# Two-layer DiT block on one core: modulation steps redistributed, first FFN weights prepared during the output projection, two more buffers where the down projection leaves its accumulators

## The chip, the cores and the metric

One core of a Trainium2 chip runs the whole forward pass as one program. The metric is the device time of that program in microseconds (us), the median of the runs shown. Engines are named as in the profile: PE (TensorE, with its weight loads PEld), DVE (VectorE), ACT (ScalarE), POOL (GpSimd), SP (SyncE, here the queue that issues nearly all DMA transfers). L12 is line 12 of the kernel before.

## What is computed

The reference is two transformer layers on 1024 tokens of width 1024 plus, in layer 0, 256 context tokens. A conditioning vector gives six modulation vectors a layer (`mod = silu(c) @ w_mod + b_mod`): shift, scale and gate of the mixer, shift, scale and gate of the FFN.

```python
for li in range(2):
    sh1, sc1, ga1, sh2, sc2, ga2 = split(silu(c) @ w_mod[li] + b_mod[li], 6)
    u = rmsnorm(h, g_norm1[li]) * (1 + sc1) + sh1
    y = mixer(u)                              # layer 0: RG-LRU + MLA, layer 1: differential attention
    h = h + ga1 * y                           # y ends with the output projection
    u = rmsnorm(h, g_norm2[li]) * (1 + sc2) + sh2
    a, g = split(u @ w_up, 2)                 # 1024 -> 2 x 2816
    h = h + ga2 * ((gelu(dwconv(g)) * a) @ w_down)
# layer 0 does the same for the context tokens, with modulation from c_ctx
```

## The kernel before, in words

Every product is made in split precision: an operand is cut into a rounded high part (a CAST on ACT, L284) and the rest (a subtraction on DVE, L99), and `mm3` (L114) issues three matmuls for one (lines 117, 118, 119). So each new weight costs ACT about one us and DVE about 1.2 us before PE can use it.

**Output projection** (`out_proj`, L790). Ten token tiles of 128 rows in layer 0 (context first), eight in layer 1. Per tile: 48 matmuls (`ops`), times the gate vector `ga` on DVE (L825), plus the residual on POOL (L826), stored; then, some stages later (`norm`, L833), the RMS norm (`scaled`: square on ACT, power on POOL L127, scaling on POOL L261), eight transposes on PE (`turned`, L271) and the writing of the FFN's input columns. Both `ga` vectors are loaded at the start (L800). In layer 0 two modulation chunks (10 and 11 of layer 0, the FFN's gate) are computed here on DVE, 16 multiply-adds each (L195). At the last tile `fill` calls `begin`: in layer 0 `ctx_first` (L964) makes the context's products of FFN tiles 0 and 1, in layer 1 `first_products` (L973) one product each for tiles 0 and 1 from half weights.

**Up projection** (`ffn_up`/`up_sequence`, L999, L1009). 22 tiles f of 128 hidden columns. The 1024 input rows and 1024 tokens are cut 2 x 2, and seven products of 12 matmuls replace eight: p1, E with operand 22, p6 (operand t2), E with t1, B with t3, A with 21, B with t4. This stretch is in `manual_schedule`: every engine gets its instructions in the order in which the code emits them. Tile 0 stands ahead of the loop (L1068 to L1102): it fetches and splits its weights, makes the weight sums (`up_sums`, L985, four DVE additions), and splits the operands t2, t1, t3, 21, t4, 22 (L910), each two casts on ACT and two subtractions on DVE. The context's two products (24 matmuls each, `pC`) are made per tile in layer 0.

**Modulation steps.** `mod_chunk_dve` (L169) with `fine` is cut into six steps per chunk (`mod_steps`, L1153): clear the accumulator and issue the first load; four times multiply-add a loaded [128, 1024] piece of `w_mod` (L195: four instructions with both conditioning vectors, two with one) and issue the next load into the same single buffer `mr`; then the sum over partitions on PE (L205 or L212) and a copy. In layer 0's up projection nine chunks, that is 54 steps, hang in a list; `some_mods` takes one step at two places of each loop pass f = 1 to 21 (L1128 behind E with t1, L1138 behind B with t3), and `while mods` (L1150) takes the rest behind the loop. Three chunks more go into layer 0's down projection.

**Down projection** (`ffn_down`, L1158). Rounds of up to four token tiles; in a round PE accumulates 22 weights for each tile in PSUM (`acc`). At the end of a round DVE multiplies each accumulator with the gate into `dtmp` (L1232, two buffers), POOL adds the residual (L1233), and the result is stored. The next round needs the same accumulators and split weights.

**Layer 1's front** (`layer1_front`, L1241). Six weight blocks in turn, ten token tiles each (`project`, 24 matmuls). Tiles 0 to 6 were normed in the down projection; tiles 7 to 9 are loaded (`load`), scaled (`scale`) and transposed (`norm`) here, at lags 0, 1 and 3 of a staggered loop in which `project` has lag 4.

Outside `manual_schedule` the order within an engine is set by a planner at build time, by the order of emission and its own estimate of when operands are ready. The `p2` banks of PSUM are one pool of four for products, transposes and the context's products.

Of the kernel before, what the change touches and what calls it, by code (L numbers as in the profile page):

```python
# [34 lines left out]
OMODS = (0, 3, 4, 7)  # L35
# [25 lines left out]
class K:  # L61
# [107 lines left out]
    def mod_chunk_dve(self, pool, l, ch, nctx, fine=False):  # L169
# [31 lines left out]
        ps = [self.PS.tile([P, 512], F32, tag="mp", bufs=1, name="modps")] if self.single else self.two("modps")  # L201
# [588 lines left out]
    def out_proj(self, l, w_name, tiles, get_yT, begin, units=()):  # L790

        nc, io = self.nc, self.io
        with ExitStack() as st:
# [6 lines left out]
            gas = [self.ga(O, l, 0, c, f"ga{c}") for c in range(2 if l == 0 else 1)]  # L800
# [4 lines left out]

            mods = [self.mod_chunk_dve(O, 0, ch, 2) for ch in (10, 11)] if l == 0 else []

            def mod(t):
                if mods and t in OMODS:
                    next(mods[OMODS.index(t) // 2], None)  # L810

            def product(t):
# [12 lines left out]
                nc.vector.tensor_mul(h[t], ps.rearrange("p a b -> p (a b)"), gas[t >= NTX])  # L825
                nc.gpsimd.tensor_tensor(h[t], h[t], xt, op=ADD)  # L826
# [20 lines left out]
            self.staggered(tiles, (load, 0), (product, 1 + l), (fill, LAG_N + l), (norm, LAG_N + l), (mod, 1))  # L847
# [67 lines left out]
    def fetch_up(self, l, f):  # L915
        raws = []
        for i in (f, NF + f):
# [46 lines left out]
    def ctx_first(self, F, n):  # L964

        for f in range(n):
            a, g = (self.split_new(x) for x in self.fetch_up(0, f))
# [5 lines left out]
    def first_products(self, F, n):  # L973

        for f in range(n):
            raw = self.W.tile([P, 1024], F32, tag="wr", bufs=NWR, name="wr")[:, :512]
            self.nc.sync.dma_start(raw, self.io["ffn_up"][1, f, :, :512])
            w = self.split_new(raw, F, "pw", 1)
            ps = self.two("p1")[0]
            for k in range(4):  # L980
                self.mm3(ps, [y[:, k * P:(k + 1) * P] for y in w], [y[:, k] for y in self.right["11"]], k == 0, k == 3)
# [17 lines left out]
    def ffn_up(self, l, F0, nfirst, chunks):  # L999


        with ExitStack() as st:
            self.PS = self.ps(st, f"psU{l}")
            self.single = True
            with self.tc.manual_schedule():
                self.up_sequence(l, st, nfirst, chunks)
            self.single = False

    def up_sequence(self, l, st, nfirst, chunks):  # L1009
# [7 lines left out]
        step, mods = {}, []  # L1017
# [81 lines left out]
        N["raw"] = self.up_sums(B, raws)  # L1099
# [3 lines left out]
        mods += [x for ch in chunks for x in self.mod_steps(F, 1, ch, 2 if ch < 4 else 1)]  # L1103
        for f in range(1, NF + 1):
# [17 lines left out]
            here = l == 0 and f >= nfirst  # L1122
# [5 lines left out]
            some_mods()  # L1128
            if here:
                cgc = self.ctx_gate(F, f, X["c"][:, :CTX])  # L1130
            if f + 1 < NF:
                N = step[f + 1] = {"a": self.split_new(raws[0])}
                if l == 0 and f + 1 >= nfirst:
                    N["a21"] = self.split_new(raws[1][:, h], F, "a21", 1)
                N["raw"] = self.up_sums(B, raws)
# [579 lines left out]
```

## Time and profile before

| | |
|---|---|
| runs | 3 |
| median | 3470.52 us |
| lowest to highest | 3469.31 to 3471.54 us |
| the profiled execution | 3466.52 us |
| its span, first to last instruction | 3464.7 us |
| granted TensorE clock, mean | 0.968 |
| bytes moved | 435.64 MB, mean 126 GB/s |

The profiled execution's time is 1.8 us more than its span, and 4.0 us below the median. A row of a timeline has the start, the duration, the engine, line, operation and operands, how many were merged, and in brackets how long the engine had been idle and who released it. The stages on the timeline: attention of layer 0 to 731, output projection 740 to 889, up projection to 1466, a stretch behind its loop to 1523, down projection to 1860, layer 1's front to 2220, attention to 2640, output projection to 2764, up projection to 3212, down projection to the end.

### The profile page before, as it was taken

What the parts mean: (1) busy time and instruction counts of PE and PEld (TensorE: products, weight loads), DVE (VectorE), ACT (ScalarE), POOL (GpSimd) and SP (SyncE); (2) the same over time, 40 slices, a digit from 0 to 9 for tenths busy, and PEclk for the clock granted to TensorE, in tenths of its full rate; (3) what the DMA queues carried; (4) which work ended last, traced back from release to release, by engine and by line L of the source; (5) the groups of instructions that cost most, each with busy time, mean ns of one, the idle gap of its engine ahead of it and who ended that gap; (6) DMA issues with size and microseconds to landing.
All of it is one profiled execution on the core that took longest, in us unless ns stands there. A gap on an engine that the chain in (4) does not pass through costs nothing.

```text
span 3464.7 us, 43470 instructions
## 1 busy us (share of the span) xinstructions
PE 3173.4 (92%) x16262; PEld 2625.9 (76%) x16262; DVE 2365.8 (68%) x3380; ACT 1417.1 (41%) x2447; POOL 948.2 (27%) x658
## 2 busy tenths in 40 slices
PE   8998899989799999949997999888888889999998
PEld 4877788867588888738775887777777768888887
DVE  6468978876777766633666487499997676766443
ACT  3355766733333333212243122377764333333322
POOL 2233578864000000000022133177774300000010
PEclk9999999999899999969998999999999989999999
DMA  6224943354122222244754354644324222222553
GB/s 258 69 76 137 291 126 96 81 162 154 51 104 94 104 90 84 88 152 151 264 185 163 110 140 104 182 111 113 101 82 142 73 67 79 86 79 88 189 173 128
DMA packets 232874, 435.64 MB, mean 126 GB/s; under 512 B 21548, under 2 KB 147756, under 8 KB 230872
## 3 DMA queue, kind: packets, MB, share of 16 engines
q1 hardware_dynamic: 230792, 426.06, 38.8%
q10 hardware_dynamic: 1872, 6.82, 0.5%
q8 instruction: 128, 2.10, 0.2%
q14 instruction: 82, 0.67, 0.1%
HBM read 321.46 MB, written 111.34 MB: 125 GB/s over the span
## 4 chain that ended last, share of the span: by engine, by line
PE 54%; DVE 12%; issue 7%; DMA 3%; ACT 2%; POOL 1%; SPq 0%; DVEq 0%; ACTq 0%; POOLq 0%
PE pB L118 5%; PE pB L117 5%; PE pB L119 5%; PE acc L119 3%; PE pj L117 3%; PE pj L118 3%; PE pj L119 3%; PE acc L117 3%; PE acc L118 3%; DVE m L1453 2%; DVE p L1469 2%; PE pE L118 2%; PE pE L119 2%; PE pE L117 2%; PE ops L118 2%
## 5 line engine op out<-in xcount | busy, mean ns | idle before, releaser
L99 DVE TENSOR_TENSOR wl<-wr,wh 128x1024 fp32r<-128x1024 f32 (+2 forms) x288 | 351.2, 1229 | 95.5 <-ACT wh L284 70.6
L119 PE MATMUL acc<-wl,hh 128*128 128x512 f32 x792 | 312.2, 394 | 13.7 <-DVE wl L99 13.7
L117 PE MATMUL acc<-wh,hh 128*128 128x512 f32 x792 | 312.6, 395 | 4.5 <-DVE dtmp L1232 2.8
L118 PE MATMUL acc<-wh,hl 128*128 128x512 f32 x792 | 310.6, 392 | 0.4 <-DVE hl L99 0.3
L1233 POOL TENSOR_TENSOR ht<-ht,dtmp 128x1024 f32<-128x1024 f32 x17 | 42.0, 2497 | 823.5 <-DVE dtmp L1232 823.5
L99 POOL TENSOR_TENSOR wl<-wf,wh 128x1280 fp32r<-128x1280 f32 x64 | 221.6, 3463 | 106.9 <-ACT wh L1488 96.5
L1448 PE MATMUL S<-k,q 128*128 128x512 f32 (+1 forms) x768 | 195.7, 379 | 57.5 <-ACT p L1459 57.3
L284 ACT CAST wh<-wr 128x1024 fp32r<-128x1024 f32 (+1 forms) x224 | 223.5, 1007 | 58.7 <-DVE wr L992 50.0
L117 PE MATMUL pB<-ht,wh 128*128 128x512 f32 x528 | 210.9, 399 | 22.9 <-ACT wh L284 17.3
L284 ACT CAST hh<-hr 128x512 fp32r<-128x512 f32 (+1 forms) x110 | 63.8, 580 | 363.3 <-PE acc L119 278.5
L99 DVE TENSOR_TENSOR hl<-hr,hh 128x512 fp32r<-128x512 f32 (+1 forms) x110 | 73.1, 665 | 203.5 <-ACT hh L284 203.2
L118 PE MATMUL pB<-ht,wl 128*128 128x512 f32 x528 | 210.0, 398 | 0.9 <-DVE wl L99 0.9
L119 PE MATMUL pB<-lt,wh 128*128 128x512 f32 x528 | 209.3, 396 | 0.0
L178 POOL MEMSET macc<- 128x512 f32 x24 | 12.4, 526 | 679.5 <-PE modps L205 438.3
L1459 ACT ACTIVATE p<-S,m 128x1280 f32<-128x1280 f32 x128 | 170.8, 1334 | 59.7 <-DVE m L1453 56.7
L1453 DVE TENSOR_REDUCE m<-S 128x1 f32<-128x1280 f32 x128 | 187.1, 1480 | 5.4 <-PE S L1448 4.7
L119 PEld LDWEIGHTS acc<-wl,hh 128*128 128x128 f32 x792 | 149.8, 189 | 51.6 <-DVE wl L99 20.6
L195 DVE SCALAR_TENSOR_TENSOR macc<-wr,sc,macc 128x512 f32<-128x512 f32 x192 | 143.3, 786 | 62.4 <-DMA wr<-w_mod 61.2
L1448 PEld LDWEIGHTS S<-k,q 128*128 128x128 f32 x768 | 123.4, 192 | 78.2 <-ACT p L1459 66.0
L117 PEld LDWEIGHTS acc<-wh,hh 128*128 128x128 f32 x792 | 150.0, 189 | 40.1 <-ACT wh L284 4.2
L117 PE MATMUL pj<-wh,u 128*128 128x512 f32 x448 | 177.2, 396 | 2.5 <-DVE qT L99 2.5
L118 PE MATMUL pj<-wh,u 128*128 128x512 f32 x448 | 177.7, 397 | 0.0
(412 smaller groups left out, 9160.0 us busy)
## 6 DMA issues: line engine op xcount, KB each, us to landing
wr<-ffn_down SPq DMA_DIRECT2D x110, 512.0 KB
wr<-ffn_up SPq DMA_DIRECT2D x92, 512.0 KB
wr<-w_mod SPq DMA_DIRECT2D x76, 512.0 KB
hid<-gc SPq DMA_DIRECT2D x44, 512.0 KB
k<-dk SPq DMA_DIRECT2D x14, 1280.0 KB
hr<-hid SPq DMA_DIRECT2D x66, 256.0 KB
wr<-w_in_c SPq DMA_DIRECT2D x24, 512.0 KB
mr<-w_mod SPq DMA_DIRECT2D x20, 512.0 KB
```

The source lines that it names most:

```text
L99: e.tensor_tensor(out, x, hi.bitcast(F32), op=SUB)
L117: mm(out, a[0], b[0], start=start, stop=False, skip_group_check=onto)
L118: mm(out, a[1], b[0], start=False, stop=False, skip_group_check=onto)
L119: mm(out, a[0], b[1], start=False, stop=stop, skip_group_check=onto)
L178: nc.gpsimd.memset(acc[c], 0.0)
L195: nc.vector.scalar_tensor_tensor(acc[c], raw[:, kk * 512:(kk + 1) * 512], self.sc[:, 2 * u + kk, c:c + 1], acc[c], op0=MUL, op1=ADD)
L284: self.nc.scalar.copy(hi, x)
L1233: (nc.vector if last else nc.gpsimd).tensor_tensor(hts[t][:, c], hts[t][:, c], tmp[:, c], op=ADD)
L1448: nc.tensor.matmul(Y["S", m][:, c0:c0 + n], heads[h]["q"][m][:, t * P:(t + 1) * P], heads[h]["k"][x, m, j], start=(x == 0), stop=(x == 1))
L1453: nc.vector.tensor_reduce(Y["m", m], Y["S", m][:, :TOK], axis=AX.X, op=ALU.max, negate=True)
L1459: nc.scalar.activation(Y["p", m], Y["S", m][:, :TOK], AF.Exp, bias=Y["m", m], accum_out=Y["s"] if m else s0[:, h, t:t + 1])
L1469: nc.vector.scalar_tensor_tensor(Y["p", 0], Y["p", 1], Y["tt"], Y["p", 0], op0=MUL, op1=ADD)
```

## The change

- The modulation chunks: layer 0's chunks 10 and 11 leave the output projection and go into layer 0's up projection, behind layer 1's chunks 0 to 3 and ahead of its chunks 4 to 6 (still nine chunks, 54 steps). Layer 1's chunks 7 to 9 instead of 9 to 11 go into the down projection, and chunks 10 and 11 into layer 1's up projection, which had none.
- The steps are spread: `per` is 54 / 20 rounded up, 3. With `per` over 2, two steps are taken behind E with t1 and one behind B with t3. In layer 1 (12 steps) one at each place. The PSUM bank `mp` gets a second buffer.
- `ga` is loaded at the first tile that uses it, into one buffer. The last tile's residual and scaling go to DVE. `xn` has one buffer in both layers.
- `begin0` and `begin1` replace `ctx_first` and `first_products`: context tile 1, then 0 (layer 0), the two first products (layer 1), and then tile 0's weight sums and all its splits, which leave `up_sequence`. In layer 1 tile 1's first weight is kept too. The `s4` split of tile 0 moves ahead of operand 22.
- `dtmp` gets four buffers. In layer 1's front `scale` has lag 4 and `norm` lag 7.

```diff
@@ mod_chunk_dve
-        ps = [self.PS.tile([P, 512], F32, tag="mp", bufs=1, name="modps")] if self.single else self.two("modps")
+        ps = [self.PS.tile([P, 512], F32, tag="mp", bufs=2, name="modps") for _ in range(nctx)] if self.single else self.two("modps")
@@ out_proj
-            gas = [self.ga(O, l, 0, c, f"ga{c}") for c in range(2 if l == 0 else 1)]
+            gas = {}
-            mods = [self.mod_chunk_dve(O, 0, ch, 2) for ch in (10, 11)] if l == 0 else []
...
-                nc.vector.tensor_mul(h[t], ps.rearrange("p a b -> p (a b)"), gas[t >= NTX])
-                nc.gpsimd.tensor_tensor(h[t], h[t], xt, op=ADD)
+                c = int(t >= NTX)
+                if c not in gas:
+                    gas[c] = self.ga(O, l, 0, c, "ga")
+                nc.vector.tensor_mul(h[t], ps.rearrange("p a b -> p (a b)"), gas[c])
+                (nc.vector if t == tiles[-1] else nc.gpsimd).tensor_tensor(h[t], h[t], xt, op=ADD)
...
-                xn = O.tile([P, D], F32, tag="xn", bufs=1 + l, name="xn")
+                xn = O.tile([P, D], F32, tag="xn", bufs=1, name="xn")
-                self.scaled(O, h[t], xn, junk)
+                self.scaled(O, h[t], xn, junk, eng=nc.vector if t == tiles[-1] else None)
...
-            self.staggered(tiles, (load, 0), (product, 1 + l), (fill, LAG_N + l), (norm, LAG_N + l), (mod, 1))
+            self.staggered(tiles, (load, 0), (product, 1 + l), (fill, LAG_N + l), (norm, LAG_N + l))
@@ in place of ctx_first and first_products
+    def begin0(self, F):
+        pair = lambda raws: [self.split_new(x) for x in raws]
+        def ctx(f, a, g):
+            ps = self.two("cg")
+            self.ctx_product(ps[0][:, :CTX], self.halves(g))
+            self.ctx_product(ps[1][:, :CTX], self.halves(a))
+            self.ctx_last(f, self.ctx_gate(F, f, ps[0][:, :CTX]), ps[1][:, :CTX])
+        ctx(1, *pair(self.fetch_up(0, 1)))
+        raws = self.fetch_up(0, 0)
+        g, a = pair(raws[::-1])
+        ctx(0, a, g)
+        self.begun = {0: {"a": a, "raw": self.up_sums(F, raws)}}
+        self.begun[0].update(g=self.split_new(raws[1]), s=self.split_13(self.begun[0]["raw"]))
+        self.fetched = None
+    def begin1(self, F):
+        def p1(f, a):
...
+            self.p1[f] = F.tile([P, 512], F32, tag=f"p1{f}", name="p1")
+            self.nc.scalar.copy(self.p1[f], ps)
+            return a
+        raws = self.fetch_up(1, 0)
+        self.begun = {0: {"a": p1(0, self.split_new(raws[0])), "raw": self.up_sums(F, raws)}}
+        self.begun[0].update(g=self.split_new(raws[1]), s=self.split_13(self.begun[0]["raw"]))
+        self.fetched = self.fetch_up(1, 1, (0,))
+        self.begun[1] = {"a": p1(1, self.split_new(self.fetched[0]))}
@@ up_sequence
-        raws = self.fetch_up(l, 0)
         X = banks(0)
-        if X["p1"] is None:
-            X["a"] = self.split_new(raws[0])
         p1(X)
         p1_out(X)
         self.split_columns(U, "t2")
-        X["raw"] = self.up_sums(B, raws)
-        X["g"] = self.split_new(raws[1])
         p6(X)
         self.split_columns(U, "t1")
-        X["s"] = self.split_13(X["raw"])
         product(X["E"], X["s"], 0, "t1", True)
-        if X["p1"] is not None:
-            X["a"] = self.split_new(raws[0])
-        raws = self.fetch_up(l, 1)
+        raws = (self.fetched or self.fetch_up(l, 1, (0,))) + self.fetch_up(l, 1, (1,))
...
-        N = step[1] = {"a": self.split_new(raws[0])}
+        N = step.setdefault(1, {})
+        if "a" not in N:
+            N["a"] = self.split_new(raws[0])
+        s4(X)
         self.split_columns(U, "22")
         self.quarters[0].close()
-        s4(X)
...
-        mods += [x for ch in chunks for x in self.mod_steps(F, 1, ch, 2 if ch < 4 else 1)]
+        mods += [x for ch in chunks for x in self.mod_steps(F, *ch)]
+        per = -(-len(mods) // (NF - 2))
...
             some_mods()
+            if per > 2:
+                some_mods()
@@ ffn_down
-                            tmp = F.tile([P, D], F32, tag="dtmp", bufs=2, name="dtmp")
+                            tmp = F.tile([P, D], F32, tag="dtmp", bufs=4, name="dtmp")
@@ layer1_front
-                self.staggered(items, (early(load), 0), (early(scale), 1), (early(norm), 3), (project, 4), (finish, 5), (first_head, 8))
+                self.staggered(items, (early(load), 0), (early(scale), 4), (early(norm), 7), (project, 4), (finish, 5), (first_head, 8))
@@ build
-                self.ffn_up(0, F0, 2, range(9))
+                self.ffn_up(0, F0, [(1, ch, 2) for ch in range(4)] + [(0, ch, 2) for ch in (10, 11)] + [(1, ch, 1) for ch in range(4, 7)])
-            self.ffn_down(0, [range(0, 4), range(4, 7), range(7, NT)], lambda t: self.h1_d[t], range(9, 12), columns)
+            self.ffn_down(0, [range(0, 4), range(4, 7), range(7, NT)], lambda t: self.h1_d[t], range(7, 10), columns)
-                self.ffn_up(1, F0, 2, ())
+                self.ffn_up(1, F0, [(1, ch, 1) for ch in (10, 11)])
```

## Rows read from the trace of the kernel before

**Rows 1.** The page's line of busy time by engine.

```profile
PE 3173.4 (92%) x16262; PEld 2625.9 (76%) x16262; DVE 2365.8 (68%) x3380; ACT 1417.1 (41%) x2447; POOL 948.2 (27%) x658
```

**Rows 2.** Busy time by stretch: length, PE, PEld, DVE, ACT, POOL, clock, DMA, GB/s.

```profile
937.00:1466.00 529.00, 528.75 (x2788) 448.62 (x2788) 380.49 (x511) 165.14 (x245) 5.26 (x10) 1.00 0.26 93
1466.00:1523.00 57.00, 3.24 (x15) 3.22 (x15) 20.88 (x27) 5.76 (x7) 0.53 (x1) 0.53 0.50 175
1860.00:1895.00 35.00, 11.15 (x49) 9.79 (x50) 21.19 (x40) 8.36 (x15) 15.00 (x11) 0.72 0.52 168
1895.00:2220.00 325.00, 321.56 (x1463) 261.81 (x1463) 193.38 (x436) 63.35 (x131) 82.31 (x80) 1.00 0.44 128
2816.00:3212.00 396.00, 395.94 (x1730) 324.28 (x1728) 270.21 (x308) 137.38 (x183) 0.00 (x0) 1.00 0.26 85
```

**Rows 3.** Timeline of PE behind the loop of layer 0's up projection.

```profile
1465.37 0.39 PE L119 MATMUL pE<-l,wh 128*128 128x512 f32 x1
...
1521.59 1.84 PE L205 MATMUL modps<-ones,macc 128*128 128x1 f32 x8 [20.48 <-DVE macc L195]
1523.29 0.77 PE L117 MATMUL acc<-wh,hh 128*128 128x512 f32 x1
```

**Rows 4.** Timeline of PE at the same hand-over in layer 1.

```profile
3213.23 0.50 PE L119 MATMUL acc<-wl,hh 128*128 128x512 f32 x1 [1.29 <-DVE wl L99]
```

**Rows 5.** Timeline of DVE behind the loop: a step that follows a step.

```profile
1510.27 1.54 DVE L195 SCALAR_TENSOR_TENSOR macc<-wr,sc,macc 128x512 f32<-128x512 f32 x2 [3.27 <-DMA wr<-w_mod]
```

**Rows 6.** Timeline of one pass of layer 0's up projection: PE, DVE and SP.

```profile
1054.36 0.39 PE L117 MATMUL pB<-h,wh 128*128 128x512 f32 x1
...
1071.05 1.84 PE L205 MATMUL modps<-ones,macc 128*128 128x1 f32 x16
...
1056.13 1.23 DVE L99 TENSOR_TENSOR wl<-s,wh 128x1024 fp32r<-128x1024 f32 x1 [1.86 <-ACT wh L284]
...
1063.59 2.73 DVE L195 SCALAR_TENSOR_TENSOR macc<-wr,sc,macc 128x512 f32<-128x512 f32 x4
...
1063.10 0.33 SPq L1118 DMA_DIRECT2D hid<-gc  x1
```

**Rows 7.** Timeline of PE in layer 0's output projection, its waits.

```profile
739.98 0.80 PE L117 MATMUL ops<-wh,yh 128*128 128x512 f32 x1 [9.14 <-ACT yh L284]
...
841.30 1.11 PE L271 MATMUL ntp<-ident,xn 128*128 128x128 f32 x4 [2.42 <-POOL xn L261]
```

**Rows 8.** Timeline of PE where the two up projections begin.

```profile
905.48 0.80 PE L117 MATMUL pB<-ht,wh 128*128 128x512 f32 x1 [7.03 <-ACT wh L284]
...
936.95 0.80 PE L117 MATMUL pB<-ht,wh 128*128 128x512 f32 x1 [2.22 <-ACT p L1056]
...
2774.29 0.80 PE L117 MATMUL pB<-ht,wh 128*128 128x512 f32 x1 [10.24 <-ACT wh L284]
...
2805.97 0.63 PE L117 MATMUL pB<-ht,wh 128*128 128x512 f32 x1
```

**Rows 9.** The end of a round: tile dtmp's waits, then DVE, POOL, PE.

```profile
  POOL ht L1233: 9.6, 8
...
1649.85 3.37 DVE L99 TENSOR_TENSOR wl<-wr,wh 128x1024 fp32r<-128x1024 f32 x1
...
1653.61 1.21 DVE L99 TENSOR_TENSOR wl<-wr,wh 128x1024 fp32r<-128x1024 f32 x1
...
1642.41 9.73 POOL L1233 TENSOR_TENSOR ht<-ht,dtmp 128x1024 f32<-128x1024 f32 x4 [140.71 <-DVE dtmp L1232]
...
1653.27 0.55 PE L119 MATMUL acc<-wl,hh 128*128 128x512 f32 x1 [2.66 <-DVE wl L99]
```

**Rows 10.** Timeline of PE, then DVE, at the start of layer 1's front.

```profile
1879.00 3.53 PE L271 MATMUL ntp<-ident,x 128*128 128x128 f32 x16 [19.05 <-DVE x L261]
...
1892.98 1.94 PE L271 MATMUL ntp<-ident,x 128*128 128x128 f32 x8 [4.85 <-DVE x L261]
...
1862.79 3.23 DVE L99 TENSOR_TENSOR wl<-wr,wh 128x1024 fp32r<-128x1024 f32 x1
```

More of the change, by code (lines that the diff above doesn't have):

```diff
@@ L804, in load @@
                 y[t] = get_yT(Y, t)
-            mods = [self.mod_chunk_dve(O, 0, ch, 2) for ch in (10, 11)] if l == 0 else []
-            def mod(t):
-                if mods and t in OMODS:
-                    next(mods[OMODS.index(t) // 2], None)
             def product(t):
@@ L913, in split_columns, with fetch_up @@
             self.split(self.V[x][:, i:i + 2], *(y[:, i:i + 2] for y in self.right[x]))
-    def fetch_up(self, l, f):
+    def fetch_up(self, l, f, which=(0, 1)):
         raws = []
-        for i in (f, NF + f):
+        for i in (f + NF * x for x in which):
             raw = self.W.tile([P, 1024], F32, tag="wr", bufs=NWR, name="wr")
@@ L962, in halves @@
         return [[y[:, c:c + 512] for y in w] for c in (0, 512)]
-    def ctx_first(self, F, n):
-        for f in range(n):
-            a, g = (self.split_new(x) for x in self.fetch_up(0, f))
+    def begin0(self, F):
+        pair = lambda raws: [self.split_new(x) for x in raws]
+        def ctx(f, a, g):
             ps = self.two("cg")
@@ L971, in ctx_first @@
             self.ctx_last(f, self.ctx_gate(F, f, ps[0][:, :CTX]), ps[1][:, :CTX])
[L973 to L978, printed above, removed]
+        ctx(1, *pair(self.fetch_up(0, 1)))
[7 more added lines that the diff above has]
+        def p1(f, a):
             ps = self.two("p1")[0]
             for k in range(4):
-                self.mm3(ps, [y[:, k * P:(k + 1) * P] for y in w], [y[:, k] for y in self.right["11"]], k == 0, k == 3)
+                self.mm3(ps, [y[:, k * P:(k + 1) * P] for y in a], [y[:, k] for y in self.right["11"]], k == 0, k == 3)
             self.p1[f] = F.tile([P, 512], F32, tag=f"p1{f}", name="p1")
             self.nc.scalar.copy(self.p1[f], ps)
+            return a
[4 more added lines that the diff above has]
+        self.begun[1] = {"a": p1(1, self.split_new(self.fetched[0]))}
     def up_sums(self, F, raws):
@@ L997, in split_13, with ffn_up @@
         return self.split_new(s[:, 0:2].rearrange("p a b -> p (a b)"))
-    def ffn_up(self, l, F0, nfirst, chunks):
+    def ffn_up(self, l, F0, chunks):
         with ExitStack() as st:
@@ L1005, in ffn_up, with up_sequence @@
             with self.tc.manual_schedule():
-                self.up_sequence(l, st, nfirst, chunks)
+                self.up_sequence(l, st, F0, chunks)
             self.single = False
-    def up_sequence(self, l, st, nfirst, chunks):
+    def up_sequence(self, l, st, F0, chunks):
         nc, PS = self.nc, self.PS
@@ L1016, in up_sequence @@
             nc.vector.memset(g[:, c:c + 1], 0.0)
-        step, mods = {}, []
+        step, mods = self.begun, []
         def bank(tag):
@@ L1121, in up_sequence @@
             s4(X)
-            here = l == 0 and f >= nfirst
+            here = l == 0 and f >= 2
             if here:
@@ L1132, in up_sequence @@
                 N = step[f + 1] = {"a": self.split_new(raws[0])}
-                if l == 0 and f + 1 >= nfirst:
+                if l == 0 and f + 1 >= 2:
                     N["a21"] = self.split_new(raws[1][:, h], F, "a21", 1)
-                N["raw"] = self.up_sums(B, raws)
+                N["raw"] = self.up_sums(F0, raws)
             product(X["B"], X["s"], 512, "t3", False)
@@ L1626, in build @@
                     self.AB2 = [self.mod_finish(0, 1, c) for c in range(2)]
-                    self.out_proj(0, "w_out_ab", [*range(NTX, NT), *range(NTX)], self.yT0, lambda: self.ctx_first(F0, 2))
-                self.ffn_up(0, F0, 2, range(9))
+                    self.out_proj(0, "w_out_ab", [*range(NTX, NT), *range(NTX)], self.yT0, lambda: self.begin0(F0))
+                self.ffn_up(0, F0, [(1, ch, 2) for ch in range(4)] + [(0, ch, 2) for ch in (10, 11)] + [(1, ch, 1) for ch in range(4, 7)])
                 self.ctx_columns.close()
             columns = st.enter_context(ExitStack())
-            self.ffn_down(0, [range(0, 4), range(4, 7), range(7, NT)], lambda t: self.h1_d[t], range(9, 12), columns)
+            self.ffn_down(0, [range(0, 4), range(4, 7), range(7, NT)], lambda t: self.h1_d[t], range(7, 10), columns)
             with ExitStack() as s2:
@@ L1644, in build @@
                     self.AB2 = [self.mod_finish(1, 1, 0)]
-                    self.out_proj(1, "w_out_c", range(NTX), self.yT1, lambda: self.first_products(F0, 2), self.first["w"])
-                self.ffn_up(1, F0, 2, ())
+                    self.out_proj(1, "w_out_c", range(NTX), self.yT1, lambda: self.begin1(F0), self.first["w"])
+                self.ffn_up(1, F0, [(1, ch, 1) for ch in (10, 11)])
             self.ffn_down(1, [range(0, 4), range(4, NTX)], lambda t: out[0, t * P:(t + 1) * P, :], (), None)
```

3 lines of the change are left out of this document (1 added, 2 removed).

## The prediction

> **What bounds the kernel.** I read the page's busy line first, then the stretches between stages, then PE's timeline at each hand-over. The busy line has PE at 92% [rows 1]. By stretch it is fuller still: layer 0's up projection 528.75 of 529 us, layer 1's 395.94 of 396, layer 1's front from 1895 on 321.56 of 325, all at clock 1.00 [rows 2]. So nothing that only frees another engine inside these loops is worth anything: what can be won are the places where PE stands. There are two large ones. Behind layer 0's loop PE works 3.24 of 57 us, at clock 0.53; at the start of layer 1's front 11.15 of 35, at 0.72 [rows 2]. Smaller ones lie at the output projections, the starts of the up projections and the ends of the down projection's rounds [rows 7 to 9]. A median is taken as the profiled execution's 3466.5 us plus 4.0. Below, + means time won.
>
> **a. The stretch behind the loop.** PE's last product of the loop ends at 1465.8 and the first `acc` starts at 1523.3: 57.5 us [rows 3]. The steps left in the list run there one behind the other: a step's two multiply-adds take 1.54 us and then wait 3.27 us for the next load into the single `mr` buffer [rows 5]; PE waits 20.48 us for the last accumulator [rows 3]. Before, 42 of 54 steps find a place in the 21 passes; with three a pass all 54 are gone after 18. What is late next is the down projection's first weight. The same hand-over in layer 1, which has no steps behind its loop, costs PE 1.29 us [rows 4]. The products that run at half clock after the stop give back about 1.7 us (the last `modps` row: 1.84 us for eight columns, as long as sixteen in the loop [rows 3, 6]); the `modps` products themselves move into the loop, 2 us of PE. 57.5 − 1.3 + 1.7 − 2 = **+56**; 44 if the first weights come 12 us late (they are issued only when `W` buffers come free), 57 at best.
>
> **b. The moved steps.** Each multiply-add step costs DVE 2.73 us with two conditioning vectors, and nothing of PE [rows 6]. With three steps a pass, a two-vector chunk takes two passes: clear, step 0, step 1; then step 2, step 3, sum. Two come back to back behind E with t1. In the first pass step 0 stands directly behind the clear, whose load SP issues only behind the store of `hid`, 8.7 us after the pass's first product, and behind two bias rows; DVE arrives there at +9.2 [rows 6]. A load takes about 3.3 us [rows 5], so DVE stands some 4.7 us. In the second pass step 3 waits 3.3 us for the load that step 2's end lets go. Queued behind the waiting step on DVE are the context's gate, the next tile's splits, its weight sums and the addition that frees a B bank; who waits for them is PE. In the second pass the place is exact: step 3 ends at 9.2 + 2.7 + 3.3 + 2.7 = +18 (DVE lags up to 2 more by the added work), while PE comes to the `modps` products at +16.7 [rows 6]: PE stands 1.3 to 3.3 us. For five chunks 3.3 each, and 8.3 (4.7 + 3.6) for the first, whose first pass has no context products ahead to cover DVE: **−25** in all. The bounds: 5 us lost, if DVE's idle time (1.86 us at one place of a pass [rows 6]) takes the waits in; 45, if each of twelve passes loses 3.3 and PE's clock falls a few times with it, as it does after the long stops [rows 2]. One-vector chunks, 1.5 us a step [rows 5], I cost at nothing: DVE's idle time in passes without context products hides them; if it doesn't, 1 us each. On SP three loads a pass stand where two did; SP issues one in 0.33 us [rows 6] and is otherwise idle: nothing.
>
> **c. Layer 0's output projection.** Out go 32 multiply-adds with two vectors each pair on DVE, eight `w_mod` loads, four bias rows and the two gate loads that SP issues ahead of the first `y`. PE first waits 9.14 us there, for a cast of `y`, and once 2.42 for POOL's scaling [rows 7]. Two 512 KB loads fewer ahead of `y` are worth 3 us of the first (one takes about that alone [rows 5], two beside each other not twice that); the 2.42 goes, and about 1.6 of half clock after it: **+7**. Bounds: 3 (only the start) and 9. Loading `ga` at its first use puts it behind the first product on SP: DVE's gate multiply waits for it, PE has other banks to go on with: nothing, or 2 us lost.
>
> **d. The start of layer 0's up projection.** p6 of tile 0 starts at 905.5 after a 7.03 us wait for a weight's cast, that of tile 1 at 936.95 [rows 8], 31.5 us apart, where a loop pass takes 25 (529 us for 21 [rows 2]). The weight sums (four additions of half a split's columns, some 0.65 us each), two whole splits at 1.23 [rows 6] and a half go from DVE's chain of operand splits into the time of the output projection's last normings: 7 us, and PE's 7.03 wait. The chain of six operand splits itself stays, and so does PE's wait for the last normed tile. DVE's residual and scaling for the last tile replace POOL's there: 1.2 us by DVE's row for a subtraction of as many columns against 2.43 by POOL's [rows 6, 9]. **+12**; 5 if the operand splits alone set the pace, 17 at most. The context's tile 1 ahead of tile 0 only changes names.
>
> **e. Four `dtmp` buffers.** DVE waits for POOL eight times, 9.6 us in all; at the round's end POOL's four additions take 9.73 us, the wl behind them 3.37 us, the next 1.21, and PE waits 2.66 [rows 9]. With four buffers the accumulators are free and DVE is past its four multiplies 2.3 us earlier. I take 2 us for each of three round ends and 1.5 at the end of the kernel: **+8**, between 1 and 10. The row speaks for a collision, though: the 3.37 us is 2.16 over the price of a split, nearly one POOL addition (9.73 / 4). The Trainium skill's page "SBUF — State Buffer", section "Who interferes with whom", says that a DVE instruction with two inputs in SBUF and a GpSimd instruction that reads SBUF block each other for whole instructions. By that rule the splits, now issued earlier, would wait for POOL's additions all the same, and e would be 1.5 or less; the 3.37 us agrees with it.
>
> **f. Layer 1's front.** PE waits 19.05 us and 4.85 us for DVE's scaled tiles before its transposes [rows 10], since the order puts norm(7) and norm(8) ahead of the first projections. At lags 4 and 7 the projections of tiles 0 to 2, normed already, come first: 3 x 24 matmuls at 0.22 us each (321.56 us for 1463 [rows 2]) are 16 us, and tile 7's load and scaling, which were through 19 us after PE's last product, lie beside them. What is late next is the fourth weight split, which ends at 1866.0 [rows 10], some 6 us behind PE's end in the down projection; only the last quarter of a product's matmuls needs it, so about 2 us stay. 19 + 4.9 − 2 + 1.5 (clock 0.72 in this stretch [rows 2]) − 1.5 for later small waits: **+22**. Bounds: 8 if the scaled tile 7 still stands ahead on some engine, 26.
>
> **g. The start of layer 1's up projection.** p6 of tile 0 waits 10.24 us for a cast; that of tile 1 comes 31.7 us later [rows 8]. Sums and three splits leave DVE's chain, as in d, and tile 1's first weight is ready. `xn` loses a buffer, so the norming of the last tiles stands closer in a row, about 4 us later for tile 6, but not for the last. **+8**, from 2 to 11. **h. Twelve steps new to layer 1's up projection**: DVE is 270 of 396 us busy [rows 2], which hides them; PE gains two sums of one 512-column matmul each, under 0.8 us by the nearest row [rows 3]: **−1.5**. If DVE's waits for `mr` reach PE, −8. The down projection's three chunks change their number only: nothing.
>
> **The sum**: 56 − 25 + 7 + 12 + 8 + 22 + 8 − 1.5 = 86.5, so 3380 us for a profiled execution and 3384 as median.
>
> **The rivals.** *The steps' waits are absorbed*: DVE catches up in its idle time and PE's products stand far enough ahead; b is −8 and the median 3367. For it: DVE is busy 380 of 529 us [rows 2]. Against: 42 steps run there already, and the twelve more come back to back. *The hand-overs keep part of their waits*: the first down weights come 12 us late (3396), or the front's order of work stays as it was, 22 lost (3406). For it: an order that the planner sets can differ from that of emission. *The port collision*: if the splits behind the multiplies and POOL's additions wait for one another, DVE is through no earlier than POOL's last addition, as now; the three round ends win nothing, e falls from 8 to 1.5, and the median is 3391; the 3.37 us speaks for it, PE's short 2.66 against its mattering [rows 9]. *The change doesn't do what it says*: steps are left behind the loop, or the last step's sum still holds PE; a is a few us, the median about 3438. *Slower*: DVE becomes the bound of tiles 1 to 18. Each pass adds a third step (2.73) and a wait (3.3 to 4.7), and if DVE has nothing free, PE loses all of it, with the clock falling after each stop: it decides from (86.5 + 25) / 18 = 6.2 us lost a pass. At 4.9 of waiting plus 2 at half clock, 18 passes lose 124 us, and the median is 3470.5 + 124 − 111.5 = 3483. Against it: 149 of 529 us of DVE are idle [rows 2], and the step's own work fits there.
>
> **How the numbers follow.** The forecast has 0.53, the absorbed waits 0.13, remaining hand-over waits 0.20, the port 0.08, the change not working 0.03, slower 0.03. The range: the forecast's own unknowns (b 20 either way, f and a 12 downwards, d and g 6) and the cases on either side, 3356 to 3412; the far cases, and the worst ends of several terms together, are the 2 in 10 left out. A measurement of this kernel can tell about 0.2%, 7 us, from no change: faster 0.95, same 0.02 (a half-working change with costly waits), slower 0.03.
>
> **What would show it.** Behind the loop PE should have a gap of one or two us in place of 57.5, and no multiply-adds there. In passes 1 to 12 DVE should wait for `w_mod` at L195, and PE before every second pass's `modps` 1 to 4 us, with clock 1.00 otherwise. At the front, projections should start within 3 us of the last `acc`, and transposes follow later. POOL's wait for `dtmp` should vanish while the wl behind it shrinks or not: that decides e. It is wrong if the up projection's loop grows by more than 45 us, or if PE still waits over 10 us at either hand-over.

## The result and the profile after

The changed kernel takes 3430.17 us (median of four runs, 3423.26 to 3431.70) against 3469.91: a ratio of 0.9882, 95% interval 0.9865 to 0.9899. That is 40 us faster, less than half of the 86 forecast and outside the range. The profiled execution is the one of 3431.70 us, the longest of the four, with a span of 3429.9; that of the kernel before (3466.52 us) is shorter than any of the four behind its median. So the two traces lie 34.8 us apart, not 40.

The page's line of busy time, which answers to [rows 1] (lines are those of the changed kernel, L99 is now L98, L195 is L194, L284 is L283):

```profile
PE 3186.3 (93%) x16262; PEld 2633.3 (77%) x16262; DVE 2360.9 (69%) x3381; ACT 1412.1 (41%) x2444; POOL 945.2 (28%) x654
```

PE has the same 16262 matmuls, yet 12.9 us more busy time: some of them run slower than before. Where, the busy times by stretch show (columns as in [rows 2]):

```profile
938.00:1492.00 554.00, 534.54 (x2736) 450.48 (x2735) 391.33 (x534) 158.76 (x239) 6.83 (x13) 0.97 0.27 94
1492.00:1506.00 14.00, 0.84 (x5) 0.38 (x3) 4.77 (x6) 2.62 (x3) 0.00 (x0) 0.62 0.63 212
1019.80:1027.60 7.80, 7.77 (x41) 7.77 (x42) 6.24 (x10) 2.90 (x5) 1.05 (x2) 0.57 0.01 2
...
1845.00:1880.00 35.00, 30.69 (x132) 24.37 (x131) 19.45 (x41) 9.60 (x18) 13.09 (x9) 0.95 0.58 200
1880.00:2185.00 305.00, 301.56 (x1383) 245.83 (x1382) 194.90 (x435) 61.73 (x129) 84.93 (x83) 1.00 0.47 133
```

The stretch behind the loop has shrunk from 57 us to 14, and the first 35 us of layer 1's front hold 30.69 us of PE instead of 11.15. But the loop, which PE filled before, is longer and now has 19 us of holes and a clock of 0.97. A ledger by stage, from PE's timelines of both profiled executions (S is the score product of the attention):

| from ... to | before, us | after, us | won | forecast |
|---|---|---|---|---|
| start to first `ops` of layer 0 | 740.0 | 736.9 | 3.1 | |
| to the end of its last transposes | 150.1 | 145.4 | 4.7 | c, with the row above: 7 |
| to p1 of tile 2 | 62.6 | 55.9 | 6.7 | d: 12 |
| to the loop's last product | 513.1 | 554.6 | -41.5 | b, and `modps` moved in: -27 |
| to the first `acc` | 57.5 | 13.1 | 44.4 | a, without `modps`: 58 |
| to the last `acc` | 336.7 | 339.7 | -3.1 | e: 6 |
| layer 1's front, to the first S | 360.5 | 339.7 | 20.8 | f: 22 |
| attention, to the first `ops` of layer 1 | 421.1 | 421.4 | -0.3 | |
| to the end of the last transposes | 122.5 | 128.7 | -6.1 | |
| to the first `acc` of layer 1 | 447.3 | 441.9 | 5.3 | g and h, with the row above: 6.5 |
| to the end | 253.4 | 252.7 | 0.7 | e: 1.5 |

Four rows carry the error: the loop (14 us), the hand-over behind it (14), the round ends (10), and layer 1's output projection (7, g and h). The start of layer 0's up projection adds 5. Each row is one execution against one: in the three kernels of experiments 7 to 9, which leave the start as it was before, the first row reads 737.0 to 739.9 us, so a us or two in a row says nothing by itself.

**The loop.** One pass of the changed kernel, tile 4: PE, then DVE, then SP, as in [rows 6].

```profile
1019.83 2.63 PE L204 MATMUL modps<-ones,macc 128*128 128x1 f32 x16 [2.54 <-DVE macc L194]
1022.32 0.56 PE L116 MATMUL pC<-uc,wh 128*128 128x256 f32 x1
1022.68 0.41 PE L117 MATMUL pC<-uc,wl 128*128 128x256 f32 x1
...
1027.59 0.46 PE L116 MATMUL pA<-h,wh 128*128 128x512 f32 x1
1027.89 0.39 PE L117 MATMUL pA<-h,wl 128*128 128x512 f32 x1
...
1011.62 2.73 DVE L194 SCALAR_TENSOR_TENSOR macc<-wr,sc,macc 128x512 f32<-128x512 f32 x4
1017.70 2.74 DVE L194 SCALAR_TENSOR_TENSOR macc<-wr,sc,macc 128x512 f32<-128x512 f32 x4 [3.35 <-DMA wr<-w_mod]
...
1014.38 0.33 SPq L183 DMA_DIRECT2D wr<-w_mod  x1
```

Step 2 ends, SP issues the load for step 3 into the same buffer, DVE stands 3.35 us, step 3 takes 2.74, and PE stands 2.54 us for it. Then comes what the forecast didn't price: the `modps` products take 2.63 us instead of 1.84, and the 24 `pC` products behind them are 0.21 us apart instead of 0.12. The granted clock is 0.57 over the stretch from 1019.8 to 1027.6 in the table above: 1.00 until 1020.8, then 0.50, PE's lower level of 1.2 GHz, from 1020.9 to 1027.6. The pass takes 32.75 us, 5.9 more than the 26.87 of such a pass before. The sums of tiles 4 to 12 wait like this, 2.5 to 3 us each, and that of tile 2, the first, 4.95 (its pass takes 37.34 us).

**Behind the loop.** PE's first product of the down projection, then SP and ACT:

```profile
1505.92 0.80 PE L116 MATMUL acc<-wh,hh 128*128 128x512 f32 x1 [13.16 <-ACT wh L283]
...
1439.86 0.37 SPq L1178 DMA_DIRECT2D wr<-ffn_down  x1
...
1496.57 0.32 SPq L1119 DMA_DIRECT2D hid<-gc  x1
1497.00 1.19 SPq L244 DMA_DIRECT2D ga<-ga  x2
1498.60 0.32 SPq L1181 DMA_DIRECT2D hr<-hid  x1
...
1504.31 0.62 ACT L283 CAST hh<-hr 128x512 fp32r<-128x512 f32 x1 [9.02 <-DMA hr<-hid]
```

SP takes the last store of `hid`, waits for it until 1496.57, then issues two gate loads, and only then the columns of `hid` that the down projection begins with. They land 5.7 us later. The first weight itself had been issued long before, at 1439.86; what is late are its columns of `hid`, which ACT casts ahead of it. This wait stood in the trace before as well, under the steps. DVE's row there:

```profile
1480.04 1.23 DVE L99 TENSOR_TENSOR wl<-wr,wh 128x1024 fp32r<-128x1024 f32 x1 [0.25 <-ACT wh L284]
```

It is the first split of a down weight, 14.3 us behind PE's last product at 1465.76. No step had to be there for PE to stand that long.

**The end of a round.** DVE, POOL and SP at the first one, as in [rows 9], PE behind it, and a later row of DVE:

```profile
1625.10 5.30 DVE L1235 TENSOR_TENSOR dtmp<-acc,ga 128x1024 f32<-128x1024 f32 x4 [4.07 <-PE acc L118]
1630.32 1.27 DVE L98 TENSOR_TENSOR hl<-hr,hh 128x384 fp32r<-128x384 f32 x1
1631.51 3.41 DVE L98 TENSOR_TENSOR wl<-wr,wh 128x1024 fp32r<-128x1024 f32 x1
1634.84 2.75 DVE L98 TENSOR_TENSOR hl<-hr,hh 128x384 fp32r<-128x384 f32 x1
...
1626.40 10.76 POOL L1236 TENSOR_TENSOR ht<-ht,dtmp 128x1024 f32<-128x1024 f32 x4 [270.13 <-DVE dtmp L1235]
...
1637.60 0.38 SPq L1178 DMA_DIRECT2D wr<-ffn_down  x1
...
1634.97 0.50 PE L118 MATMUL acc<-wl,hh 128*128 128x512 f32 x1 [1.30 <-DVE wl L98]
...
1644.74 0.50 PE L116 MATMUL acc<-wh,hh 128*128 128x512 f32 x1 [1.73 <-ACT wh L283]
1647.59 0.79 PE L117 MATMUL acc<-wh,hl 128*128 128x512 f32 x1 [2.35 <-DVE hl L98]
...
1645.53 1.54 DVE L194 SCALAR_TENSOR_TENSOR macc<-wr,sc,macc 128x512 f32<-128x512 f32 x2 [6.82 <-DMA wr<-w_mod]
```

The four multiplies run without a pause now, and every split behind them collides with a POOL addition: three are slowed where two were, and POOL's four additions take 10.76 us instead of 9.73. SP, whose queue holds the stores that wait for POOL, issues the next weight 12.5 us after the first multiply; before it was 11.5. PE's third wait, 2.35 us, has another cause: the `hl` split that it waits for stands on DVE behind a modulation step (last row), which waited 6.82 us for its load.

**The starts and the front.** PE's waits at p1 of layer 0's tile 0, at the front's first transposes, and at the second last transposes of layer 1's output projection, with the square on ACT that begins their tile's norming:

```profile
887.34 0.80 PE L116 MATMUL pB<-h,wh 128*128 128x512 f32 x1 [5.08 <-DVE gc L954]
...
1867.10 1.68 PE L270 MATMUL ntp<-ident,x 128*128 128x128 f32 x8 [4.31 <-DVE rs_t L130]
...
2725.15 1.97 PE L270 MATMUL ntp<-ident,xn 128*128 128x128 f32 x8 [7.39 <-POOL xn L260]
...
2717.86 1.06 ACT L257 ACTIVATE xn<-tmp 128x1024 f32<-128x1024 f32 x1 [6.97 <-PE ntp L270]
```

The front's 19.05 us [rows 10] have become 4.31, as forecast. But p1 waits for a row that had kept nobody waiting: DVE's last multiply of the context's tile 0, which reads a PSUM bank. And the norming in layer 1 waits for the one `xn` buffer: ACT's square, which writes to it, stands until PE has transposed the tile before.

### The profile page after: what moved, and what is told of

Same layout as the page of the kernel before. It is cut to its first block, busy times and chain, and to the rows that moved or that the text cites. A ratio compares the mean times of both kernels' runs of the same rounds, so it can differ in the third digit from the quotient of the medians.

```text
span 3429.9 us, 43450 instructions
## 1 busy us (share of the span) xinstructions
PE 3186.3 (93%) x16262; PEld 2633.3 (77%) x16262; DVE 2360.9 (69%) x3381; ACT 1412.1 (41%) x2444; POOL 945.2 (28%) x654
## 3 DMA queue, kind: packets, MB, share of 16 engines
q10 hardware_dynamic: 1872, 6.82, 0.6%
## 4 chain that ended last, share of the span: by engine, by line
PE 54%; DVE 14%; DMA 3%; issue 3%; ACT 3%; POOL 1%; SPq 0%; DVEq 0%; ACTq 0%; POOLq 0%
PE acc L118 4%; PE pB L116 4%; PE pB L118 4%; PE pB L117 4%; PE acc L116 4%; PE acc L117 4%; DVE m L1456 3%; PE pj L116 3%; PE pj L117 3%; PE pj L118 3%; DVE p L1472 3%; PE pE L118 2%; PE pE L116 2%; PE pE L117 2%; PE ops L117 2%
## 5 line engine op out<-in xcount | busy, mean ns | idle before, releaser
L98 DVE TENSOR_TENSOR wl<-wr,wh 128x1024 fp32r<-128x1024 f32 (+2 forms) x285 | 348.8, 1233 | 92.9 <-ACT wh L283 63.4
L283 ACT CAST wh<-wr 128x1024 fp32r<-128x1024 f32 (+1 forms) x221 | 220.9, 1008 | 83.4 <-DVE wr L999 72.4
L98 POOL TENSOR_TENSOR wl<-wf,wh 128x1280 fp32r<-128x1280 f32 x64 | 221.9, 3468 | 106.3 <-ACT wh L1491 94.7
L98 DVE TENSOR_TENSOR hl<-hr,hh 128x512 fp32r<-128x512 f32 (+1 forms) x110 | 76.0, 691 | 206.7 <-ACT hh L283 206.6
L194 DVE SCALAR_TENSOR_TENSOR macc<-wr,sc,macc 128x512 f32<-128x512 f32 x192 | 135.8, 748 | 105.2 <-DMA wr<-w_mod 104.1
L283 ACT CAST hh<-hr 128x512 fp32r<-128x512 f32 (+1 forms) x110 | 63.7, 579 | 325.0 <-PE acc L118 242.0
L1462 ACT ACTIVATE p<-S,m 128x1280 f32<-128x1280 f32 x128 | 170.8, 1334 | 60.6 <-DVE m L1456 57.5
```

What stands on the lines that cost most here:

```text
L98: e.tensor_tensor(out, x, hi.bitcast(F32), op=SUB)
L194: nc.vector.scalar_tensor_tensor(acc[c], raw[:, kk * 512:(kk + 1) * 512], self.sc[:, 2 * u + kk, c:c + 1], acc[c], op0=MUL, op1=ADD)
L283: self.nc.scalar.copy(hi, x)
L1462: nc.scalar.activation(Y["p", m], Y["S", m][:, :TOK], AF.Exp, bias=Y["m", m], accum_out=Y["s"] if m else s0[:, h, t:t + 1])
```

## The experiments

**1 and 2: the waiting load or the work?** Both leave the steps' work in the loop. The first cuts the loads in halves, in three buffers:

```diff
+    raw = pool.tile([P, 512], F32, tag="mr", bufs=3, name="wr")
+    nc.sync.dma_start(raw, io["w_mod"][l, ch, i // 2][:, i % 2 * 512:(i % 2 + 1) * 512])
```

> The changed kernel, with the modulation loads of both up projections cut in two and three buffers of 256 KB in place of one of 512 KB, so that most of the next step's load is under way while a step runs; the steps keep their places. Theory 1 (what holds PE in every second pass is the 3.35 us that DVE waits between step 2 and step 3 for a load into the single buffer, and the fall of the clock after that stop): the seven passes with a sum of a two-vector chunk fall from 31 to 37 us to 25 to 27, no wait of PE ahead of modps stays over 0.5 us, about 40 us are won, near 3390 us. Rival (a third step is simply too much work for DVE between E with t1 and modps: two steps of 2.73 back to back): PE still waits 2 us or more ahead of modps and at most 15 us are won, 3415 us or more.

The second keeps the one buffer and moves a step:

```diff
+            if per > 2 and f < NF:
+                some_mods()
             self.convolved(l, f - 1, g, gc, SEQ)
...
             some_mods()
-            if per > 2:
-                some_mods()
```

> The changed kernel with its single buffer, but the two steps behind E with t1 are not back to back: the first of the three steps of a pass is taken ahead of the convolution (after p1 is copied out), one behind E with t1, one behind B with t3. Theory 1 (the wait for the load, not the work): each load has more than 5 us between two steps, the passes come back to 25 to 27 us, about 40 us won, near 3390 us; at most a us or two goes to the store of hid, 2.7 us later. Rival (the work of a third step on DVE): DVE is as loaded as before, PE waits somewhere else in each pass for 2 us or more, and less than 15 us are won.

Measured: 3398.69 us for the halves (ratio 0.9797, 0.9781 to 0.9814), 3395.15 for the places (0.9779, 0.9764 to 0.9793). With separate places, the timeline of the same pass, PE and then DVE:

```profile
1008.80 1.84 PE L204 MATMUL modps<-ones,macc 128*128 128x1 f32 x16
...
995.02 2.73 DVE L194 SCALAR_TENSOR_TENSOR macc<-wr,sc,macc 128x512 f32<-128x512 f32 x4
...
1003.99 2.74 DVE L194 SCALAR_TENSOR_TENSOR macc<-wr,sc,macc 128x512 f32<-128x512 f32 x4
```

And the busy times of its loop, from p1 of tile 2 on:

```profile
939.92:1451.00 511.08, 510.94 (x2710) 431.68 (x2709) 385.43 (x523) 158.36 (x237) 6.84 (x13) 1.00 0.29 101
```

DVE has the same work and waits for a load once, 0.4 us, PE stands nowhere in the loop, the clock is 1.00. The rival (the third step's work) falls: a step more in a pass costs PE nothing but the `modps` products (the loop takes 517.5 us, 4.4 more than before, with two more chunks of two vectors in it), two back to back over one buffer cost 35 us by the medians. The halves leave only the first chunk's wait, 1.69 us, for which no load can be ahead: 33.33 us for that pass and 27 for the others.

**3: two `dtmp` buffers again** (`bufs=4` to `bufs=2`).

> The changed kernel with two dtmp buffers again, nothing else. By the forecast's term e (four buffers win 2 us at each of three round ends and 1.5 at the end) it is 7 us slower than the changed kernel, the layer-0 down projection 346 us from its first to its last product. By the rival of the collision (DVE's splits and POOL's additions hold each other up, so that POOL's last addition and the weight loads queued on SP behind the stores come no earlier with four buffers) it is 0 to 3 us faster, 337 to 340 us.

Measured: 3424.45 us (3423.72 to 3425.02). That is inside the changed kernel's own spread (3423.26 to 3431.70), so no difference is shown in the total. By stage, layer 0's down projection takes 338.5 us instead of 339.7; but the other runs here with four buffers and POOL's additions (experiments 1, 2, 5, 6, 10) take 338.0 to 341.4, so that loss isn't shown. From layer 1's first `acc` to the end it is 254.5 instead of 252.7, and 250.9 to 252.6 in those runs: at the kernel's end, where no splits follow, four buffers win about 2. What never varies is when SP issues the next weight at the first round's end: 11.5 us behind the first multiply with two buffers, 12.5 with four, in every run with POOL's additions. The 8 us of term e are not there.

**4: the additions on DVE**, behind the next round's first split.

```diff
...
+    for ht, tmp, to in later:
+        nc.vector.tensor_tensor(ht, ht, tmp, op=ADD)
+        nc.sync.dma_start(to, ht)
```

> The changed kernel, with the residual's additions at the end of a round that has a next one taken from POOL and put on DVE behind the next round's first split, the stores with them. Collision theory: no split shares its time with POOL; hl and wl take 0.55 and 1.21 us in place of 1.3 to 3.4 and run directly behind the four multiplies, SP issues the next weights ahead of the stores, PE's waits of 1.3, 1.7 and 2.4 us at the first round's end fall to under 1 in all, the layer-0 down projection takes about 334 us in place of 339.7: 5 us won, and 1 or 2 more in layer 1. Rival (the waits are those of the weight and hid loads themselves, which share the DMA with the modulation loads): they stay, and nothing is won within 2 us.

Measured: 3424.17 us (3418.11 to 3425.75; ratio 0.9860, 0.9845 to 0.9875), again not clear of the changed kernel's spread; the down projection 338.1 us, where 334 was expected. The timeline of DVE, then PE's first waits, then SP:

```profile
1628.16 0.55 DVE L98 TENSOR_TENSOR hl<-hr,hh 128x384 fp32r<-128x384 f32 x1
1628.62 1.22 DVE L98 TENSOR_TENSOR wl<-wr,wh 128x1024 fp32r<-128x1024 f32 x1
1629.76 4.62 DVE L1222 TENSOR_TENSOR ht<-ht,dtmp 128x1024 f32<-128x1024 f32 x4
...
1639.78 1.54 DVE L194 SCALAR_TENSOR_TENSOR macc<-wr,sc,macc 128x512 f32<-128x512 f32 x2 [3.80 <-DMA wr<-w_mod]
1641.24 0.55 DVE L98 TENSOR_TENSOR hl<-hr,hh 128x384 fp32r<-128x384 f32 x1
...
1636.04 0.50 PE L118 MATMUL acc<-wl,hh 128*128 128x512 f32 x1 [0.45 <-DVE wl L98]
1641.85 0.50 PE L117 MATMUL acc<-wh,hl 128*128 128x512 f32 x1 [1.62 <-DVE hl L98]
...
1635.87 0.62 SPq L1178 DMA_DIRECT2D wr<-ffn_down  x1
```

Without POOL beside them the splits take 0.55 and 1.22 us instead of 1.27 and 3.41, and PE's waits of 1.30, 1.73 and 2.35 us become 0.45 and 1.62. The collision is shown. What it costs in all isn't: the 1.6 us won in the stage lie within the 338.0 to 341.4 of experiment 3. Two things in the trace speak for a small gain. SP still takes the stores first, so the next weight goes out 12.9 us after the first multiply, not earlier. And the waits that stay, 1.62 us here and 2.83 at 1679.8, are for splits that stand on DVE behind a modulation step whose load is late, as in the loop: near the rival, though the load is that of `w_mod`.

**5 and 6: the hand-over.** First the first three fetches through ACT's queue, with the gates behind them; then, besides, the first weight and its columns in the last pass of the loop:

```diff
-            fetch(i)
+            fetch(i, nc.scalar if l == 0 else nc.sync)
         split(0)
+        gas = [self.ga(F, l, 1, c, f"ga{c}") for c in range(2 if l == 0 else 1)]
...
+            elif l == 0 and f + 1 == NF:
...
+                nc.sync.dma_start(w, self.io["ffn_down"][0, 0:P, :])
...
+                nc.sync.dma_start(x, self.hid_d[0, :, 0:512])
```

> The changed kernel; the first three weights of layer 0's down projection and their columns of hid are fetched through ACT's queue instead of SP's, and the two gate loads come behind them. Theory (what is left of the stretch behind the loop, 13.6 us of PE's time, is the transfer of those operands, which SP issues only behind the last store of hid and two gate loads): they are issued behind ACT's last gelu, some 3 us earlier, and share the DMA with nothing; the gap falls to 7 to 9 us, 5 us won. Rival (the operands wait for the memory of the up projection's operands, which PE's last product frees, and so come as late by any queue): the gap stays within 2 us of 13.6.

> As the run before, and the very first weight with its columns of hid is fetched in the last pass of the up projection into memory of its own, ahead of the last store of hid. Theory (transfer and order on SP): its cast and split need only ACT, behind the gelu; PE starts 4 to 6 us after its last product instead of 13.6, and may wait again, 1 to 3 us, for the second weight: 8 to 10 us won against the changed kernel. Rival (the memory that hh and hl are written into comes free late): the gap stays over 10 us.

Measured: 3422.20 us (3416.17 to 3423.76) and 3419.17 (3414.33 to 3426.30), 8 and 11 us by the medians, beside a spread of 8 in the changed kernel's own runs. PE's first `acc` in the timeline of the one with ACT's queue alone:

```profile
1501.11 0.79 PE L116 MATMUL acc<-wh,hh 128*128 128x512 f32 x1 [5.79 <-ACT wh L283]
```

And in that with the first weight ahead:

```profile
1493.64 0.79 PE L116 MATMUL acc<-wh,hh 128*128 128x512 f32 x1 [4.42 <-ACT wh L283]
```

13.16 us become 5.79 (7 to 9 were expected) and 4.42: the wait was transfer and order on SP, not memory that came free late. The queue and the place of the gate loads weren't tried apart. What is left at the end is ACT's gelu of the last tile and two casts.

**7: the same wait in the kernel before.** A third place for a step alone, ahead of the convolution, added to the kernel before, so that nothing stands behind its loop.

> The kernel before with a third place for a step in each pass of layer 0's up projection, ahead of the convolution, so that all 54 steps are gone after 18 passes; nothing else. By the forecast's term a and no loss b, 54 to 56 us would be won, 3415 us. By the reading of the trace before (the first weight of the down projection is split on DVE at 1480.0, 14 us behind PE's last product, whether steps stand there or not) PE still waits 13 to 15 us behind the loop, and 41 to 44 us are won, 3427 us.

Measured: 3431.67 us (ratio 0.9887, 0.9873 to 0.9902), and PE behind the loop:

```profile
1480.53 0.79 PE L117 MATMUL acc<-wh,hh 128*128 128x512 f32 x1 [13.19 <-ACT wh L284]
```

So this one edit wins as much as the whole change did (39.7 us; 41 to 44 were expected by the row at 1480.04), and the 13 us remain in a kernel with none of its other parts, as that row said.

**8: one `xn` buffer in the kernel before.**

> The kernel before, with one xn buffer in layer 1 too, nothing else of the change. The forecast had this cost the second last tile 4 us and the last none, so nothing in the end. By the reading of the trace after (from PE's last product of layer 1's output projection to its last transposes 18.4 us instead of 12.8), it costs 5 to 6 us, all of it there.

Measured: 3473.47 us against 3471.89 (ratio 1.0008, 0.9999 to 1.0018), but from layer 1's last `ops` to the end of the last transposes 17.2 us instead of 12.8. At its place it costs 4.4 us, a little less than expected (6.2 from the first `ops` on, 128.7 for 122.5); the total can't tell it from nothing, nor from 6.

**9: the front's lags alone in the kernel before.**

> The kernel before with the two lags of layer 1's front alone (scale 4, norm 7). By the forecast's term f it wins 22 us, 3450 us, and the front from its last acc before to its last projection takes 339 us instead of 360.6. Rival (part of that gain belongs to other parts of the change, such as the modulation chunks that left the down projection's end): it wins less than 15.

Measured: 3447.14 us (ratio 0.9930, 0.9914 to 0.9947), 24 us won; from the last `acc` to the first S 338 us instead of 360.5. Term f stands on its own.

**10: the context's first products a tile earlier** (`if t == tiles[-1]` to `tiles[-2 + l]` ahead of `begin`).

> The changed kernel, with the context's two first products and the first splits of layer 0's up projection emitted one tile earlier in the output projection. Theory (the first product p1 waits 5.1 us for DVE's last multiply of the context's tile 0, which reads the bank that p1 writes, and this is why term d came out half): with the gate chain a tile earlier, p1 follows PE's last transposes within 1.5 us, and 4 to 6 us are won, 3425 us. Rival (p1 then waits as long for its own operands, or the last normings come later because the splits now stand ahead of them on DVE): nothing is won within 2 us, or it is slower.

Measured: 3413.12 us (ratio 0.9830, 0.9813 to 0.9846), 17 under the changed kernel's median and 10.1 under its fastest run. From the last `ops` of layer 0 to p1 of tile 2 it takes 70.7 us instead of 81.0. p1's wait is gone, and PE's waits ahead of the transposes are shorter too, 6.75 us for 9.43:

```profile
872.06 1.09 PE L270 MATMUL ntp<-ident,xn 128*128 128x128 f32 x8 [1.32 <-POOL xn L260]
878.58 1.94 PE L270 MATMUL ntp<-ident,xn 128*128 128x128 f32 x8 [5.43 <-DVE xn L260]
```

The direction was right, the size twice what was expected. Why the normings gain as well wasn't tried apart.

**11 and 12: the repairs together.** Separate places, additions on DVE and the first weight ahead; then the earlier context products besides.

> The changed kernel with three separate places for the steps, the additions of a round's end on DVE behind the next split, and the first down weight ahead with the others through ACT's queue. If the three causes are independent, 40 us, 3 us and 8 to 10 us add up: 3378 us. If they share a cover (DVE busier, or the DMA fuller), less than 45 us in all, 3385 us or more.

> The kernel with the three repairs together, and this one too. If it is independent of the others, 4 to 6 us under that kernel's 3376 us: 3371 us. By the rival, 3376 us or more.

Measured: 3376.44 us (ratio 0.9725, 0.9710 to 0.9740) and 3365.47 us (0.9690, 0.9676 to 0.9705). They add up: the earlier products bring 11 us on top, as many as they won by stage in experiment 10 (10.3), and more than the 4 to 6 expected. The second is 108 us faster than the kernel before (3473.24 beside it) and 65 faster than the changed one: more than the forecast had promised, with the same work in other places and orders.

## Why the prediction was wrong

**b, the moved steps: right mechanism, one term left out.** The forecast named the 3.3 us wait behind step 2, DVE's place at +18 and PE's stop of 1.3 to 3.3 us; the trace shows 3.35 and 2.5 to 3. It took 3.3 us a chunk as the whole price and kept the fall of the clock for the bound. With separate places (experiment 2) as the measure, the five passes lose 5.9, 6.0, 6.1, 4.7 and 4.3 us, since the slow stretch behind a stop costs about as much as the stop, and tile 2's loses 10.1: 37 us in place of 25. The other 4.4 us the loop with separate places has over the kernel before as well, most of it the `modps` products of two chunks more with two vectors, 1.84 us each; the forecast had 2 for them. The loop lost 41.5 us in all instead of 27; the bound of 45 for b held.

**a, the hand-over: the wrong step was "what is late next".** The forecast took layer 1's 1.29 us [rows 4] as the model and gave the late weights to a bound and a rival (0.20). In layer 1 the first operands are fetched ahead of the last store (in the trace before the columns of `hid` at 3198.92, that store at 3219.61); in layer 0 SP's order has store, gates, then the columns of `hid`. The trace of before had the answer at 1480.04. The rival with 12 us was the true case in size: 44.4 us won, experiments 5 to 7. Its reason, weights that wait for `W` buffers, was not: the first weight was issued early. Nor did the 1.7 us of half clock come back: the first `acc` products run at 0.50 for 6.1 us, and did so for 4.0 before. The forecast's own sign of being wrong, more than 10 us at a hand-over, showed.

**e, `dtmp`: the rival was right.** The forecast took 2 us for each round end because DVE would be through 2.3 us earlier. It was, by 2.0 (5.3 us for the four multiplies instead of 7.3), and ran into POOL. The Trainium skill's page "SBUF — State Buffer", section "Who interferes with whom", which the prediction weighed, agrees with the rows of experiment 4: 3.41 us beside POOL's reads, 1.22 without. What the forecast had not drawn from it: POOL is held up too (10.76 us for 9.73), and SP's fetches wait behind the stores of POOL's results, so the next weight went out a us later, not at the same time.

**g, `xn`: the wrong step was "but not for the last".** With one buffer a tile's norming waits for the transposes of the tile before, which PE makes behind its last products; from the last `ops` on that is 5.6 us in the changed kernel, 4.4 alone (experiment 8). **d** was half: DVE's chain did become shorter, but p1 now waits 5.08 us for DVE's last multiply of the context, for which it had not waited before. Experiment 10 gave it back. Whether the new order, tile 1 and then tile 0, of which the forecast said that it only changes names, is the reason, wasn't tried apart.

**c and f were right**: 7.8 for 7, and 20.8 (24 alone) for 22. **h** can't be told from g. Two rivals (late operands at the hand-over, collision) came true at once, with b near its bad end besides; the forecast gave each a chance by itself, as if only one could happen, and its range of 28 us either way could not carry errors that all pointed the same way.

## What to carry to other kernels

Before costing a removed stall at its whole length, look under it: read when the next stage's operands were ready on each engine, and which queue they stood in. Where a step frees its only buffer and the next step wants it at once, place the steps a load's time apart: here the work cost nothing, the adjacency did. And price a stop of PE inside a full loop as the stop plus the slow stretch behind it, from a row that shows such a stretch.

## What had not been expected of the hardware

In the changed kernel's loop a stop of 2.54 us ahead of `modps`, with PE otherwise full, was followed by a fall of the granted clock to the lower level: 1.00 until 1020.8, 0.50 from 1020.9 to 1027.6. In experiment 1 a fall followed a stop of 1.69 us too (0.50 from 960.8 to 967.4): `modps` took 2.26 us, and that pass 33.33 us. The length of the stop alone doesn't decide it: behind one of 2.10 us in the changed kernel's down projection the clock stayed at 1.00 (1687.44 to 1700), as it did behind one of 2.25 us from 922.46 on. What else does wasn't tried.
